# Scan products on 64-row tiles of the array with unpadded queries, and split ffn inputs moved in SBUF

## The chip, the cores and the metric

One core of a Trainium2 chip runs the whole program in one launch. The metric is device time in microseconds (us) of one execution: the median of the timed runs. A profiled execution gives the trace: a start and a duration for each instruction on TensorE (PE for matmuls, PEld for weight loads), VectorE (DVE), ScalarE (ACT), GpSimd (POOL) and SyncE (SP, which issues the DMAs).

## The reference

A two-layer backbone over 1024 latent tokens and 256 context tokens, width 1024, all in fp32. Layer 0 mixes tokens by attention and a convolution, layer 1 by a bidirectional RWKV-7 scan with 16 heads of 64; each layer ends in a SwiGLU channel mixer of hidden width 2816. What matters here is the scan and the mixer:

```python
def swiglu(h, w1, w3, w2):
    return (jax.nn.silu(h @ w1) * (h @ w3)) @ w2

def step(S, inp):                       # one token; per head a 64 x 64 state S
    w_t, k_t, v_t, kk_t, b_t = inp[:5]
    sa = jnp.einsum('bhvk,bhk->bhv', S, kk_t)
    S = S * w_t[:, :, None, :] - sa[..., None] * b_t[:, :, None, :] + v_t[..., None] * k_t[:, :, None, :]
    y = jnp.einsum('bhvk,bhk->bhv', S, inp[5]) if emit else None
    return S, y

for d in range(2):                      # forward and backward
    s_ctx, yc = wkv_scan(s0, dec_c, k_c, fc['vh'], fc['kk'], b_c, fc['r'], rev)
    _, yl = wkv_scan(s_ctx, dec_l, k_l, fl['vh'], fl['kk'], b_l, fl['r'], rev)
out_lat = rwkv_readout(y_lat[0] + y_lat[1], fl, p)   # group norm, bonus, gate, projection
```

## The kernel before, in words

**Order.** The program is written in a tile framework that allots buffers, inserts the waits, and orders the instructions of each engine from the order of the code together with its own model of their durations. The phases follow one another: the mixer of layer 0, its output projection (`mix_out`), `ffn(0)`, the projections of layer 1, `layer1_scan`, `mix_out(1)`, `ffn(1)`, `store`.

**Split products.** Large products are made in three passes: `split` makes a high part (ACT) and the remainder (DVE) of an operand, and `mm3` issues high x high, high x low and low x high (lines 59, 60 and 61). So `pf<-xh,whi` in a view is the first pass of an ffn product.

**ffn.** `ffn(l, ...)` runs over groups of two hidden blocks of 128. For each block and each token tile (`TT`: the context's 256 tokens, then two tiles of 512 latent tokens) the inputs `xh`, `xl` are multiplied with two 128-column blocks of w1 and w3 (tile `pf`); silu and product give `sl`, which is split into `gh`, `gl`; these are multiplied with w2 (also called `pf` in the views) and added to the residual `hT`. `operands(l, sizes)` allots `xh` and `xl` in a pool X0 or X1, opened before the weights' pools. In this allocation the rows of X0 and X1 begin 192 bytes past those of the weights, both taken mod 512 bytes; `gh` and `gl` lie in the weights' own pool, at distance 0. The `xh`, `xl` of 512 tokens are read in `mix_out` as well (tile `pw`).

**Scan.** The 16 heads are taken in 4 quarters Q of two head pairs (`pr`), each pair two heads (`h`) of 64. Per quarter there are five windows of 256 tokens (`g` = 0 is the context, without output; 1 to 4 the latent tokens), per window four chunks of 64 tokens (`m`), and both directions `d` run in turn. `HR[0]` and `HR[1]` are partitions 0 to 63 and 64 to 127: for most operands partitions hold the two heads of a pair, feature by feature.

- `prep_in` loads the window's operands by DMA and makes, on ACT, DVE and POOL, the scaled keys `kb` and the queries `qa` (for the correction inside a chunk) and `qz` (for the output). `qa` and `qz` are padded: for each chunk there are two blocks of 64 columns, one for each head, and the block of head h is zero on the partitions of the other. The zeros are written once (the memsets of line 1051); each window writes the two halves by one POOL op each (`pmul`, line 1056). `abp` is the 64x64 product of keys and queries that is inverted.
- `prep_mat` makes `kps`: keys by queries, 128 partitions contracted, with the zeros keeping the heads apart; then `l` on DVE (mask), and transposes of the keys (`tps` to `bk`).
- `prep_inv` inverts the triangular blocks, on DVE for the most part (lines 1203 and 1204), to `xc`.
- `scan` is the recurrence. For each chunk and direction: `px` (from `l` and the values `sv`, then from `qa` and the state `sc`), copied by ACT into `xs` with two ops (line 1267) into a block-diagonal form; `pu` = xc times xs, copied by ACT into `sv`; `pss` = new state, scaled on DVE to `sc`; then `py`, the output, from `qz` and `sc` and from `l` and `sv`. In `px` and `py` the two 64-column tiles of the array take the two pairs, each matmul contracting over all 128 rows.
- `readout` normalizes, adds the bonus (`vy`) and gates the output of a window, and transposes it by TensorE (`yps`).

The loop at the end of `layer1_scan` sets `scan` of window n beside the inversion and `kps` of window n + 1 and the loads of window n + 2, and up to two readouts.

Of the kernel before, what the change touches and what calls it, by code (L numbers as in the profile page):

```python
# [9 lines left out]
F32 = mybir.dt.float32  # L10
F32R = mybir.dt.float32r
# [32 lines left out]
class Kern:  # L44
# [942 lines left out]
    def layer1_scan(self, R, prepared):  # L987
# [5 lines left out]
        with ExitStack() as st:  # L993
# [52 lines left out]
            qas = [[U.tile([P, 8, 2, 64], F32, name=f"qa{d}{i}") for i in range(3)] for d in range(2)]  # L1046
            qzs = [[U.tile([P, 8, 2, 64], F32, name=f"qz{d}{i}") for i in range(2)] for d in range(2)]
            svs = [[U.tile([P, 2, 2, 2, 64], F32, name=f"sv{d}{i}") for i in range(2)] for d in range(2)]
            xs = [U.tile([P, 2, P], F32, name=f"xs{d}") for d in range(2)]
            for t in (xcs[0], xcs[1], xs[0], xs[1], *qas[0], *qas[1], *qzs[0], *qzs[1]):  # L1050
                nc.vector.memset(t, 0.0)
# [9 lines left out]
            def start_quarter(Q):  # L1061
# [9 lines left out]
                for pr in range(2):  # L1071
                    f0 = Q * 256 + pr * 128
                    nc.sync.dma_start(q.lg[HR[pr]].rearrange("p h v -> p (h v)"), I["rw_ln_g"][0][f0:f0 + 128].partition_broadcast(64))
# [3 lines left out]
            def prep_in(Q, q, g, n):  # L1077
# [34 lines left out]
                for d, u in enumerate(units):  # L1112
# [11 lines left out]
                    u.qa, u.qz = qas[d][n % 3], qzs[d][n % 2]  # L1124
                    for h in range(2):
                        pmul(u.qa[HR[h], :, h], rv(pprev)[HR[h]], rv(kkwin)[HR[h]])
# [23 lines left out]
                if lat:  # L1150
                    for u in units:
                        rw = u.win[2]
                        for h in range(2):
                            pmul(u.qz[HR[h], :, h], u.pcur[HR[h]], rw[HR[h]])
                        u.cq = S.tile([P, 8, 64], F32, tag="cq", name="cq", bufs=3)
                        pmul(u.cq, u.t, rw)

            def prep_mat(Q, q, g, units):
# [6 lines left out]
                for i in range(2):  # L1165
                    for d, u in enumerate(units):
                        hw, kb = i ^ d, u.kb
                        l = u.l[hw] = U.tile([P, 2, 4, P], F32, tag=f"l{d}", name="l", bufs=3)
                        for e in range(2):
                            m = 2 * hw + e  # L1170
                            ps = pk.tile([P, 4, P], F32, tag="k", name="kps")
                            for pr in range(2):
                                for c, x in ((0, u.qa), (64, u.qz))[:w // 64]:
                                    nc.tensor.matmul(ps[:, 2 * pr:2 * pr + 2, c:c + 64], kb[:, 4 * pr + m].rearrange("p a s -> p (a s)"), x[:, 4 * pr + m], start=True, stop=True)
                            nc.vector.tensor_tensor(l[:, e, :, :w], ps[:, :, :w], msk[d][:, :, :w].to_broadcast([P, 4, w]), op=ALU.mult)
# [16 lines left out]
            def prep_inv(units, par):  # L1192
# [38 lines left out]
                for d in range(2):  # L1231
                    units[d].xc = xc[:, 8 * d:8 * d + 8].rearrange("p (m h) s -> p m h s", h=2)
# [17 lines left out]
            def scan(Q, q, g, units):  # L1250
                lat = g > 0
                for j in range(4):
                    for d in range(2):
# [5 lines left out]
                        l = u.l[m // 2][:, m % 2]  # L1259
# [309 lines left out]
```

## Time and profile before

| | us |
|---|---|
| median of 3 timed runs | 4185.2 (4184.05 to 4185.81) |
| profiled execution, its own time | 4188.13 |
| its span in the trace | 4186.4 |
| PE busy | 3832.1 (92% of the span) |
| PEld busy | 3132.3 (75%) |
| DVE busy | 2403.9 (57%) |
| ACT busy | 1741.1 (42%) |
| POOL busy | 1161.3 (28%) |
| mean granted TensorE clock | 0.943 |

The stages as the trace has them, roughly: ffn of layer 0 from 970 to 1900, projections of layer 1 to 2405, scan from 2410 to 3345, output projection of layer 1 to 3430, ffn of layer 1 to 4170, store. How to read a line of the views: `L59 PE MATMUL pf<-xh,whi 128*128 128x512 f32` is line 59 of the kernel, on PE, writing pf from xh and whi, on a tile of 128 rows by 128 columns of the array, with an operand of 128 partitions by 512 columns. An fp32 matmul in the scan appears as two records; in the split products each pass is one. The duration of a matmul in the trace is a modelled one and overlaps its neighbours; the interval between starts says what one costs.

### The profile page before, as it was taken

What the parts mean: (1) busy time and instruction counts of PE and PEld (TensorE: products, weight loads), DVE (VectorE), ACT (ScalarE), POOL (GpSimd) and SP (SyncE); (2) the same over time, 40 slices, a digit from 0 to 9 for tenths busy, and PEclk for the clock granted to TensorE, in tenths of its full rate; (3) what the DMA queues carried; (4) which work ended last, traced back from release to release, by engine and by line L of the source; (5) the groups of instructions that cost most, each with busy time, mean ns of one, the idle gap of its engine ahead of it and who ended that gap; (6) DMA issues with size and microseconds to landing.
All of it is one profiled execution on the core that took longest, in us unless ns stands there. A gap on an engine that the chain in (4) does not pass through costs nothing. (4 is left out here: it accounts for less than half of the span.)

```text
span 4186.4 us, 70705 instructions
## 1 busy us (share of the span) xinstructions
PE 3832.1 (92%) x28764; PEld 3132.3 (75%) x28764; DVE 2403.9 (57%) x4577; ACT 1741.1 (42%) x3590; POOL 1161.3 (28%) x978
## 2 busy tenths in 40 slices
PE   8888899899999999997998979787887799999999
PEld 5665667688888888886887957676776578888887
DVE  5698776555333433338678378878787654333433
ACT  4446566643111111116667357666666442111111
POOL 2869554510000000004223164645544020000000
PEclk9898999999999999998999979898988899999999
DMA  4322222331111111113223222222222231111111
GB/s 174 125 86 69 74 92 72 109 109 46 41 39 33 40 41 41 36 36 99 74 95 102 79 85 70 80 70 78 75 62 65 85 111 51 46 45 51 51 46 56
DMA packets 301669, 297.07 MB, mean 71 GB/s; under 512 B 19408, under 2 KB 267872, under 8 KB 301344
## 3 DMA queue, kind: packets, MB, share of 16 engines
q1 hardware_dynamic: 293488, 277.07, 21.4%
q10 hardware_dynamic: 7056, 14.75, 1.0%
q8 instruction: 227, 3.72, 0.4%
q0 software_dynamic: 800, 0.73, 0.1%
q14 instruction: 98, 0.80, 0.1%
HBM read 246.36 MB, written 46.14 MB: 70 GB/s over the span
## 5 line engine op out<-in xcount | busy, mean ns | idle before, releaser
L59 PE MATMUL pf<-xh,whi 128*128 128x512 f32 (+1 forms) x1760 | 654.2, 372 | 0.0
L61 PE MATMUL pf<-xh,wlo 128*128 128x512 f32 (+1 forms) x1760 | 654.1, 372 | 0.0
L60 PE MATMUL pf<-xl,whi 128*128 128x512 f32 (+1 forms) x1760 | 653.8, 372 | 0.0
L54 ACT ACTIVATE whi<-raw 128x1024 fp32r<-128x1024 f32 (+1 forms) x207 | 214.8, 1049 | 909.3 <-PE pf L60 788.5
L55 DVE TENSOR_TENSOR wlo<-raw,whi 128x1024 fp32r<-128x1024 f32 (+1 forms) x207 | 270.1, 1314 | 259.6 <-ACT whi L54 254.9
L762 DVE SCALAR_TENSOR_TENSOR hT<-pf,mod,hT 128x512 f32<-128x512 f32 (+1 forms) x440 | 306.3, 697 | 196.3 <-PE pf L61 194.3
L751 DVE TENSOR_TENSOR sl<-sl,pf 128x512 f32<-128x512 f32 (+1 forms) x110 | 69.8, 635 | 581.2 <-PE pf L61 581.2
L61 PEld LDWEIGHTS pf<-xh,wlo 128*128 128x128 f32 x1760 | 330.8, 188 | 64.7
L60 PEld LDWEIGHTS pf<-xl,whi 128*128 128x128 f32 x1760 | 330.8, 188 | 64.5
L59 PEld LDWEIGHTS pf<-xh,whi 128*128 128x128 f32 x1760 | 330.6, 188 | 64.6 <-ACT xh L221 0.3
L60 PE MATMUL pf<-gl,whi 128*128 128x512 f32 (+1 forms) x880 | 324.1, 368 | 0.0
L61 PE MATMUL pf<-gh,wlo 128*128 128x512 f32 (+1 forms) x880 | 323.9, 368 | 0.0
L59 PE MATMUL pf<-gh,whi 128*128 128x512 f32 (+1 forms) x880 | 323.9, 368 | 0.0
L581 POOL TENSOR_TENSOR pl<-pe,pt 128x512 fp32r<-128x512 f32 (+1 forms) x176 | 226.4, 1297 | 190.8 <-PE po L60 103.0
L791 POOL MEMSET apad<- 128x8 f32 x4 | 0.2, 122 | 884.6 <-PE pf L61 884.6
L367 POOL TENSOR_TENSOR co<-co,cpr 128x655 f32<-128x655 f32 x90 | 193.8, 2154 | 46.6 <-ACT cpr L366 36.9
L54 ACT ACTIVATE gh<-sl 128x512 fp32r<-128x512 f32 (+1 forms) x110 | 64.9, 590 | 307.8 <-DVE sl L751 307.8
L59 PEld LDWEIGHTS pf<-gh,whi 128*128 128x128 f32 x880 | 165.9, 189 | 27.9
L60 PEld LDWEIGHTS pf<-gl,whi 128*128 128x128 f32 x880 | 165.9, 189 | 27.7
L61 PEld LDWEIGHTS pf<-gh,wlo 128*128 128x128 f32 x880 | 165.9, 189 | 27.6
L1203 DVE TENSOR_TENSOR tmp<-A,X 128x126 f32<-128x126 f32 (+22 forms) x620 | 154.0, 248 | 52.3 <-ACT X L1197 38.6
L354 DVE SCALAR_TENSOR_TENSOR co<-yp,parC,co 128x1310 f32<-128x1310 f32 (+1 forms) x90 | 177.0, 1967 | 1.5
(407 smaller groups left out, 9634.8 us busy)
## 6 DMA issues: line engine op xcount, KB each, us to landing
raw<-in_ffn_w_dram SPq DMA_DIRECT2D x132, 512.0 KB, 3.9
araw<-in_ada_w_dram SPq DMA_DIRECT2D x96, 512.0 KB, 4.5
low<-lod SPq DMA_DIRECT2D x40, 256.0 KB, 2.8
kw<-kd SPq DMA_DIRECT2D x40, 256.0 KB, 3.0
kkw<-kkd SPq DMA_DIRECT2D x40, 256.0 KB, 2.8
sv<-vd SPq DMA_DIRECT2D x80, 128.0 KB, 3.1
raw<-in_even_w_out_dram SPq DMA_DIRECT2D x16, 512.0 KB, 3.6
rw<-rd SPq DMA_DIRECT2D x32, 256.0 KB, 3.1
```

The costliest lines, as they stand in the source:

```text
L54: self.nc.scalar.activation(hi, src, AF.Copy)
L55: return self.nc.vector.tensor_tensor(lo, src, f32(hi), op=ALU.subtract)
L59: mm(ps, wh, xh, start=start, stop=False)
L60: mm(ps, wh, xl, start=False, stop=False)
L61: mm(ps, wl, xh, start=False, stop=stop)
L354: nc.vector.scalar_tensor_tensor(co, yp[:, w + c:w + c + n], cw(j, w), co, op0=ALU.mult, op1=ALU.add)
L367: nc.gpsimd.tensor_tensor(co, co, pr, op=ALU.add)
L581: nc.gpsimd.tensor_tensor(pl, pe, f32(pt), op=ALU.subtract)
L751: nc.vector.tensor_tensor(sl[:, :n], sl[:, :n], pp[1][:, :n], op=ALU.mult)
L762: nc.vector.scalar_tensor_tensor(hT[ti][:, mb], ps[:, :n], g[:, mb], hT[ti][:, mb], op0=ALU.mult, op1=ALU.add)
L791: nc.gpsimd.memset(ap[:, :, c:c + 1], 0.0)
L1203: nc.vector.tensor_tensor(tmp, A[:, k + 1:32, k:k + 1].to_broadcast([P, n, wd]), X[:, k:k + 1, 0:wd].to_broadcast([P, n, wd]), op=ALU.mult)
```

## The change

Scan:

- `qa`, `qz` and their zeros are replaced by one tile `q` per window and direction (three buffers): per chunk 64 columns of `qa` and 64 of `qz`, no padding. Each is written by one POOL op on 128 partitions in place of two on 64.
- A head's products contract over its own 64 rows: `kps` of the two heads goes to two PSUM banks through two 64x128 tiles, `abp` uses 64x32 tiles, the `q` products in `px` and `py` 64x64 tiles, `pu` 64x64 tiles. The products with `l` contract over 128 rows as before.
- Output partitions of `px`, `pu`, `py` and of the readout now stand for the head, not for the pair. So `xs` is one ACT op on 128 partitions, `yps` is made by 16 matmuls of 64x64 with a part of the identity in place of four transposes, and the loads of `vy` and of the norm's gain `lg` are four DMAs each in place of two.

ffn: `operands` puts a pad of 80 fp32 columns (modulo 128) ahead of the tiles of 512 tokens, so that their rows come to distance 0 from the weights mod 512 bytes; the tile of 256 tokens stays at 192.

The diff, cut:

```diff
-            qas = [[U.tile([P, 8, 2, 64], F32, name=f"qa{d}{i}") for i in range(3)] for d in range(2)]
-            qzs = [[U.tile([P, 8, 2, 64], F32, name=f"qz{d}{i}") for i in range(2)] for d in range(2)]
-            xs = [U.tile([P, 2, P], F32, name=f"xs{d}") for d in range(2)]
-            for t in (xcs[0], xcs[1], xs[0], xs[1], *qas[0], *qas[1], *qzs[0], *qzs[1]):
+            for t in xcs:
                 nc.vector.memset(t, 0.0)
...
-                for pr in range(2):
-                    f0 = Q * 256 + pr * 128
-                    nc.sync.dma_start(q.lg[HR[pr]].rearrange("p h v -> p (h v)"), ...)
+                for h in range(2):
+                    for pr in range(2):
+                        nc.sync.dma_start(q.lg[HR[h], pr], lng[h, pr].partition_broadcast(64))
...
-                    for h in range(2):
-                        pmul(u.qa[HR[h], :, h], rv(pprev)[HR[h]], rv(kkwin)[HR[h]])
+                    u.q = U.tile([P, 8, 2, 64], F32, tag=f"q{d}", name="q", bufs=3)
+                    pmul(u.q[:, :, 0], rv(pprev), rv(kkwin))
...
-                    for m in range(4):
-                        for b in range(4):
-                            i, c0 = 4 * (b // 2) + m, 32 * (b % 2)
-                            nc.tensor.matmul(ps[32 * b:32 * b + 32, 2 * m:2 * m + 2, 0:64 - c0], u.kb[:, i, 0, c0:c0 + 32], u.qa[:, i, :, c0:64], start=True, stop=True)
+                    for i in range(8):
+                        for b in (0, 2, 1, 3):
+                            r, c0, j = HR[b // 2], 32 * (b % 2), 2 * (i % 4) + i // 4
+                            nc.tensor.matmul(ps[32 * b:32 * b + 32, j, 0:64 - c0], u.kb[r, i, 0, c0:c0 + 32], u.q[r, i, 0, c0:64], start=True, stop=True)
...
-                        for h in range(2):
-                            pmul(u.qz[HR[h], :, h], u.pcur[HR[h]], rw[HR[h]])
+                        pmul(u.q[:, :, 1], u.pcur, rw)
...
-                        for e in range(2):
-                            m = 2 * hw + e
-                            ps = pk.tile([P, 4, P], F32, tag="k", name="kps")
-                            for pr in range(2):
-                                for c, x in ((0, u.qa), (64, u.qz))[:w // 64]:
-                                    nc.tensor.matmul(ps[:, 2 * pr:2 * pr + 2, c:c + 64], kb[:, 4 * pr + m]..., x[:, 4 * pr + m], start=True, stop=True)
-                            nc.vector.tensor_tensor(l[:, e, :, :w], ps[:, :, :w], msk[d]..., op=ALU.mult)
+                        pss = [pk.tile([P, 4, P], F32, tag="k", name="kps") for _ in range(2)]
+                        for j in range(4):
+                            c = 4 * (j % 2) + 2 * hw + j // 2
+                            for h in range(2):
+                                nc.tensor.matmul(pss[h][:, j, :w], kb[HR[h], c]..., u.q[HR[h], c]...[:, :w], start=True, stop=True)
+                        for h in range(2):
+                            nc.vector.tensor_tensor(l[:, h, :, :w], pss[h][:, :, :w], msk[d]..., op=ALU.mult)
...
-                        for h in range(2):
-                            for pr in range(2):
-                                nc.tensor.matmul(px[HR[pr], h], l[:, 2 * pr + h, 0:64], sv[:, pr, h], start=True, stop=False)
-                            for pr in range(2):
-                                nc.tensor.matmul(px[HR[pr], h], u.qa[:, 4 * pr + m, h], sc[:, pr], start=False, stop=True)
-                        for pr in range(2):
-                            nc.scalar.activation(xs[d][HR[pr], :, 64 * pr:64 * pr + 64], px[HR[pr]], AF.Copy)
-                            (pu: two matmuls of 128 columns)
+                        for pr in range(2):
+                            for h in range(2):
+                                nc.tensor.matmul(px[HR[h], pr], l[:, h, pr, 0:64], sv[:, pr, h], start=True, stop=False)
+                            for h in range(2):
+                                nc.tensor.matmul(px[HR[h], pr], u.q[HR[h], 4 * pr + m, 0], sc[HR[h], pr], start=False, stop=True)
+                        xs = U.tile([P, 2, 64], F32, tag=f"xs{d}", name="xs", bufs=2)
+                        nc.scalar.activation(xs, px, AF.Copy)
+                        for pr in range(2):
+                            for h in range(2):
+                                nc.tensor.matmul(pu[HR[h], pr], u.xc[HR[h], m, pr], xs[HR[h], pr], start=True, stop=True)
...
+                            for pr in range(2):
+                                for h in range(2):
+                                    nc.tensor.matmul(py[HR[h], pr], u.q[HR[h], 4 * pr + m, 1], sc[HR[h], pr], start=True, stop=False)
+                                for h in range(2):
+                                    nc.tensor.matmul(py[HR[h], pr], l[:, h, pr, 64:128], sv[:, pr, h], start=False, stop=True)
...
-                    nc.tensor.transpose(ps[:, m]..., yt[:, m]..., self.ident)
+                    for pr in range(2):
+                        for h in range(2):
+                            nc.tensor.matmul(ps[HR[h], m, pr], yt[HR[h], m, pr], self.ident[HR[h], HR[h]], start=True, stop=True)
...
-                xs_ = {i: [X.tile([P, KB, sizes[i]], F32R, name=f"x{k}{i}") for k in "hl"] for i in order}
+                xs_, at = {}, 0
+                for i in order:
+                    pad = ((80 if sizes[i] == 512 else 0) - at) % 128
+                    if pad:
+                        X.tile([P, pad], F32, name=f"pad{i}")
+                        at += pad
+                    xs_[i] = [X.tile([P, KB, sizes[i]], F32R, name=f"x{k}{i}") for k in "hl"]
```

More of the change, by code (lines that the diff above doesn't have):

```diff
@@ L1070, in start_quarter @@
                 q.lg = R.tile([P, 2, 64], F32, tag="lg", name="lg", bufs=2)
[L1071 to L1073 removed]
+                lng = I["rw_ln_g"][0][Q * 256:Q * 256 + 256].rearrange("(q h v) -> h q v", q=2, h=2)
+                for h in range(2):
+                    for pr in range(2):
+                        nc.sync.dma_start(q.lg[HR[h], pr], lng[h, pr].partition_broadcast(64))
                 q.y = {}
@@ L1231, in prep_inv @@
                 for d in range(2):
-                    units[d].xc = xc[:, 8 * d:8 * d + 8].rearrange("p (m h) s -> p m h s", h=2)
+                    units[d].xc = xc[:, 8 * d:8 * d + 8].rearrange("p (m q) s -> p m q s", q=2)
             cur = [None, None]
@@ L1258, in scan @@
                         sv = svt[:, m % 2]
[L1259 removed]
+                        l = u.l[m // 2][:, :, 2 * (m % 2):2 * (m % 2) + 2]
                         px = pc.tile([P, 2, 64], F32, tag=f"c{d}", name="px")
[L1261 to L1272 removed]
+                        for pr in range(2):
[5 more added lines that the diff above has]
+                        nc.scalar.activation(xs, px, AF.Copy)
+                        pu = pc.tile([P, 2, 64], F32, tag=f"c{d}", name="pu")
+                        for pr in range(2):
+                            for h in range(2):
+                                nc.tensor.matmul(pu[HR[h], pr], u.xc[HR[h], m, pr], xs[HR[h], pr], start=True, stop=True)
+                        for h in range(2):
+                            nc.scalar.activation(sv[0:64, :, h], pu[HR[h]], AF.Copy, scale=-1.0)
                         if not (g == 4 and j == 3):
@@ L1288, in scan @@
                             py = pc.tile([P, 2, 64], F32, tag="y", name="py")
-                            for h in range(2):
-                                for pr in range(2):
-                                    nc.tensor.matmul(py[HR[pr], h], u.qz[:, 4 * pr + m, h], sc[:, pr], start=True, stop=False)
-                                for pr in range(2):
-                                    nc.tensor.matmul(py[HR[pr], h], l[:, 2 * pr + h, 64:128], sv[:, pr, h], start=False, stop=True)
+                            for pr in range(2):
[3 more added lines that the diff above has]
+                                    nc.tensor.matmul(py[HR[h], pr], l[:, h, pr, 64:128], sv[:, pr, h], start=False, stop=True)
                             win = (tok - NCTX) // 256
@@ L1305, in readout @@
                 vy = R.tile([P, 4, 2, 64], F32, tag="vy", name="vy", bufs=1)
-                for pr in range(2):
-                    f0 = Q * 256 + pr * 128
-                    nc.sync.dma_start(vy[HR[pr]].rearrange("p m h v -> p m (h v)"), self.vd[NCTX + win * 256:NCTX + (win + 1) * 256, f0:f0 + 128].rearrange("(m t) f -> t m f", t=64))
+                vin = self.vd[NCTX + win * 256:NCTX + (win + 1) * 256, Q * 256:Q * 256 + 256].rearrange("(m t) (q h v) -> h q t m v", t=64, q=2, h=2)
+                for h in range(2):
+                    for pr in range(2):
+                        nc.sync.dma_start(vy[HR[h], :, pr], vin[h, pr])
                 gt = R.tile([P, 2, 256], F32, tag="gt", name="gt", bufs=1)
@@ L1326, in readout @@
                 for m in range(4):
-                    for pr in range(2):
-                        nc.tensor.matmul(ps[HR[pr], 2 * m:2 * m + 2], q.cr[win][:, 64 * m:64 * m + 64], selh[:, pr], start=True, stop=True)
+                    for h in range(2):
+                        nc.tensor.matmul(ps[HR[h], 2 * m:2 * m + 2], q.cr[win][:, 64 * m:64 * m + 64], selh[:, :, h], start=True, stop=True)
                 cf = R.tile([P, 8], F32, tag="cfs", name="cfs", bufs=2)
@@ L1336, in readout @@
                 for m in range(4):
-                    nc.tensor.transpose(ps[:, m].rearrange("p a t -> p (a t)"), yt[:, m].rearrange("p h v -> p (h v)"), self.ident)
+                    for pr in range(2):
+                        for h in range(2):
+                            nc.tensor.matmul(ps[HR[h], m, pr], yt[HR[h], m, pr], self.ident[HR[h], HR[h]], start=True, stop=True)
                 for pr in range(2):
```

9 lines of the change are left out of this document (2 added, 7 removed).

## The prediction, made before the change was timed

> **What bounds the kernel now.** I read the page from the top: the busy shares, the granted clock by slice, and the chain that ended last.
>
> ```profile
> span 4186.4 us, 70705 instructions
> ...
> PE 3832.1 (92%) x28764; PEld 3132.3 (75%) x28764; DVE 2403.9 (57%) x4577; ACT 1741.1 (42%) x3590; POOL 1161.3 (28%) x978
> ...
> PEclk9898999999999999998999979898988899999999
> ...
> PE pf L59 6%; PE pf L61 6%; PE pf L60 6%; DMA out_dram<-o 0%; PE t L1429 0%; PE cps L186 0%; ACT o L1431 0%; PE cpb L193 0%; DVE hT L762 0%; ACTq L1431 0%
> ```
>
> TensorE is busy 92% of the span, and the end is a chain of nothing but pf matmuls, the ffn of layer 1. That share is an average over stages, so I took busy time by stage: ffn of layer 0, the scan, ffn of layer 1. Columns: length, then PE, PEld, DVE, ACT, POOL busy, granted TensorE clock, DMA share, GB/s.
>
> ```profile
> 1000.00:1800.00 800.00, 800.00 (x4157) 679.95 (x4156) 290.50 (x409) 120.83 (x174) 0.00 (x0) 1.00 0.13 39
> 2410.00:3345.00 935.00, 758.57 (x12576) 626.09 (x12576) 727.78 (x2085) 589.93 (x1530) 443.49 (x401) 0.87 0.25 73
> 3500.00:4160.00 660.00, 660.00 (x2856) 534.44 (x2855) 237.85 (x294) 106.78 (x138) 0.00 (x0) 1.00 0.15 45
> ```
>
> In both ffn stages PE is never idle and the clock is whole: there the time is the sum of matmul intervals, and what an interval loses the kernel loses. The scan is otherwise: PE is idle for 935 - 759 = 176 us, DVE is busy 728, the clock is 0.87. It is a chain that hops between engines, and PE time there counts in part. The two halves of the change fall into these two kinds of stage.
>
> **The ffn operands, term by term.** Matmuls in order of start, each start and its modelled duration; the start-to-start interval is the price.
>
> ```profile
> 3691.49 0.39 PE L61 MATMUL pf<-gh,wlo 128*128 128x512 f32 x1
> ...
> 3703.05 0.39 PE L61 MATMUL pf<-gh,wlo 128*128 128x512 f32 x1
> 3703.27 0.39 PE L59 MATMUL pf<-xh,whi 128*128 128x512 f32 x1
> ...
> 3714.47 0.39 PE L59 MATMUL pf<-xh,whi 128*128 128x512 f32 x1
> ```
>
> From gh (the second product; gh lies in the weights' pool, its rows at distance 0 from them mod 512 bytes) 51 intervals take 11.56 us: 226.7 ns. From xh (rows 192 bytes past the weights) 48 take 11.20 us: 233.3 ns. Same shape, line and clock; the operand's place is what differs. The padding moves the 512-wide xh and xl to distance 0, so I price them like gh: 233.3 - 226.7 is 6.6 ns less, of which I take 6.4, as the starts are read to 10 ns. The number moved:
>
> ```profile
> L59 PE MATMUL pf<-xh,whi 128*128 128x512 f32 x1408 | 556.9, 396 | 0.0
> L59 PE MATMUL pw<-xh,whi 128*128 128x512 f32 x224 | 90.5, 404 | 3.5 <-ACT whi L54 3.5
> ```
>
> Three products each (lines 59, 60, 61): 3 x 1408 = 4224 in the ffns, 3 x 224 = 672 in the output projections, 4896 x 6.4 ns = 31 us. PE has no idle time there to swallow it: **-31 us** in full. Bounds: 0 if distance isn't the cause, -32 at 6.6 ns. The 256-wide context tile is left at 192, and there the order is the reverse: from gh 47 intervals take 5.63 us, 119.8 ns.
>
> ```profile
> 1040.07 0.28 PE L59 MATMUL pf<-gh,whi 128*128 128x256 f32 x1
> ...
> 1045.70 0.28 PE L61 MATMUL pf<-gh,wlo 128*128 128x256 f32 x1
> ...
> 1012.53 0.28 PE L59 MATMUL pf<-xh,whi 128*128 128x256 f32 x1
> ...
> 1017.64 0.28 PE L59 MATMUL pf<-xh,whi 128*128 128x256 f32 x1
> ```
>
> From xh 45 take 5.11 us, 113.6. So the distance isn't simply good or bad, and leaving this tile where it is costs nothing.
>
> **The scan.** Its groups: records, busy us, mean ns, idle time before and its releaser (an fp32 matmul shows as two records).
>
> ```profile
> L1174 PE MATMUL kps<-qa,kb 128*128 128x128 f32 x640 | 147.4, 325 | 22.3 <-DVE l L1175 15.4 <-ACT cr L1190 4.4 <-ACT bk L1181 2.0
> L1174 PE MATMUL kps<-qz,kb 128*128 128x128 f32 x512 | 110.8, 302 | 2.7 <-POOL qz L1056 2.7
> L1267 ACT ACTIVATE xs<-px 64x128 f32<-64x128 f32 x320 | 86.9, 272 | 87.2 <-PE px L1265 81.8 <-ACT xs L1267 0.4
> L1056 POOL TENSOR_TENSOR qa<-pp,kkw 64x512 f32<-64x512 f32 x79 | 95.0, 1202 | 24.6 <-ACT pp L1118 20.8 <-DMA sv<-vd 0.7
> L1056 POOL TENSOR_TENSOR qz<-pp,rw 64x512 f32<-64x512 f32 x64 | 84.4, 1320 | 84.3 <-PE py L1291 82.1
> L1056 POOL TENSOR_TENSOR kp<-kkw,pi 128x512 f32<-128x512 f32 x39 | 51.2, 1313 | 3.8 <-DVE gneps L1025 1.1
> ```
>
> And the stretch that prices a record and a change of tile:
>
> ```profile
> 2603.79 0.39 PE L1174 MATMUL kps<-qz,kb 128*128 128x128 f32 x2
> 2604.01 0.39 PE L1174 MATMUL kps<-qa,kb 128*128 128x128 f32 x2
> 2604.33 0.34 PE L1291 MATMUL py<-sc,qz 128*64 128x64 f32 x4
> 2604.49 0.29 PE L1293 MATMUL py<-sv,l 128*64 128x64 f32 x4
> 2604.61 0.29 PE L1291 MATMUL py<-sc,qz 128*64 128x64 f32 x4
> ```
>
> *kps, gain.* Two records take 0.22 us, so 640 + 512 = 1152 take 127 us. Afterwards the padding's zero half is gone: two matmuls on 64-row tiles, in two PSUM banks, do in one pass what took two. If the tiles run side by side, half goes: **-63 us of PE time**; if not, 0.
>
> *Change of tile, cost.* The two kps records begun at 2604.01 would be done at 2604.23; py, on 128x64 tiles, starts at 2604.33, and its first four records take 0.16 where the next four take 0.12. That is 0.10 + 0.04, about 0.145 us, for one change of tile shape. The nearest row for a change of row tile:
>
> ```profile
> 1986.35 0.28 PE L61 MATMUL p3m<-mh,wlo 128*128 128x256 f32 x1
> 1986.56 0.38 PE L915 MATMUL p3b<-rh,hexp 16*128 16x256 f32 x1
> 1986.78 0.28 PE L916 MATMUL p3b<-rl,hexp 16*128 16x256 f32 x1
> 1986.99 0.39 PE L59 MATMUL p3m<-mh,whi 128*128 128x256 f32 x1
> 1987.21 0.28 PE L60 MATMUL p3m<-ml,whi 128*128 128x256 f32 x1
> 1987.33 0.28 PE L61 MATMUL p3m<-mh,wlo 128*128 128x256 f32 x1
> ```
>
> Five intervals take 0.98 where five of the usual 0.118 would be 0.59: 0.39 more for two changes, 0.19 each. Afterwards l keeps 128x64 tiles while the q product takes 64x64, in turn: px goes l, q, l, q (3 changes within), py goes q, l, q, l (3). There are 4 quarters x 5 windows x 4 chunks x 2 directions = 160 px and 128 py, so 3 x 288 = 864 changes where none were: x 0.145 = **+125 us of PE time**. I take 0.145, from tiles of the same width; bounds 0 (no row shows 128x64 against 64x64) and 0.19, +164. Beside that pu becomes 64x64 and pss stays 128x64: at most one more change in each of 160 steps, +23, kept for the upper end.
>
> The Trainium skill, page "TensorEngine Tiling (Array Packing)", section "Key Properties", says that changing the tiling mode, not just the tile, drains the TensorE, which speaks against this change; the trace agrees by the 0.145 and 0.19 above. By that rule all 864 are paid, which is rival C's 4252 if none of it is hidden; by the lower bound none is, which is rival B's 4145.
>
> *Smaller PE terms.* yps: 4 transposes become 16 matmuls of two records.
>
> ```profile
> L1337 PE MATMUL yps<-ident,yw 128*128 128x128 f32 x64 | 10.9, 296 | 2.2 <-DVE yw L1333 2.1
> ...
> 2662.61 0.69 PE L1228 MATMUL gp<-xc,gz 32*32 32x32 f32 x32
> ```
>
> Four transposes at 0.11 are 0.44 us; 32 records, four in 0.117 as in py, are 0.93: +0.5 x 16 = +8. abp has twice the matmuls of half the length: the same columns. If issue bounded it, 1280 more records at the 0.69 / 32 = 0.0216 us of the smallest tiles are +28; I take 0, since the column stream sets the interval elsewhere. pu doubles its matmuls and halves their columns: 0.
>
> *Sum on PE:* -63 + 125 + 8 = +70 at full clock, /0.87 = +80. *What reaches the end:* at least nothing (176 us of PE idle could take it), at most all. px sits on the recurrence (ACT's xs waits 81.8 us on it), yet work of the other direction fills much of a wait; I take half: **+40**.
>
> *ACT.* xs becomes one op of 128 partitions: 320 x 0.272 to 160 x 0.272, -43 us of ACT. The pair's second op lies on the recurrence, and half of its pairs overlap other waits; 80 serial steps x 0.272 = 22 bounds it; the PE changes are late next, and with the other direction running beside it I take a quarter: **-6**.
>
> *DVE and POOL.*
>
> ```profile
> L1051 DVE MEMSET qa<- 128x1024 f32 x6 | 5.5, 912 | 5.9 <-PE p3m L61 5.2 <-issue 0.7
> ...
> 2404.91 0.87 SPq L1091 DMA_DIRECT2D rw<-rd  x2
> ```
>
> Ten memsets of 0.912 us go, ahead of the scan on DVE; they run while the first chunk is loaded and projected: **-3**, bounds 0 and -9. POOL: a half op takes as long as a whole one (1.2 to 1.3 us, kp 1.31), so 80 + 64 ops become 40 + 32, about -90 us. Nothing but 2.7 us of kps waits on qz, so this is hidden: 0. The 82.1 us that qz waits for py goes too, with three buffers for both halves; kb's wait for its own buffer is late next on POOL, and nobody waits for POOL there.
>
> *DMA issues.* vy 32 to 64, lg 8 to 16, half as large, on SP: 40 more at 0.87 / 2 = 0.44 us, 18 us of SP over 935, ahead of the sv and window loads in the queue. These are issued a chunk or more ahead: 0, at worst some us.
>
> **Sum.** -31 + 40 - 6 - 3 = 0 against the profiled execution's own 4188.1 us (span 4186.4 and 1.7 around it). The median of the timed runs is 4185.2, 3 us lower; so **4185 us**.
>
> **Rivals.** (B) *The changes of tile are hidden.* PE idles 176 us in the scan, and the drain may overlap the wait that follows anyway; or 128x64 to 64x64 doesn't drain. Then PE's terms give nothing or a gain: -31 - 9 = -40, 4145; with half the kps share also reaching the end (-63 / 0.87 / 2 = -36), 4109. For it: the idle time, and DVE's 728 us as the other bound. Against: the 0.10 that py waited in the middle of ready work. (C) *The changes are paid in full*, since each px is on the recurrence of its direction and both directions make them: (70 + 23) / 0.87 = 107, less 9, less 31: +67, 4252. It decides against the change once more than (31 + 9) / 107 = 37% of the added PE time reaches the end. For it: xs's wait on px. (D) *The two row tiles of kps don't run side by side*, so that half isn't saved: PE +133 / 0.87 / 2 = +76 instead of +40, 4221. No row here shows two 64-row tiles at once; 32x32 tiles do run so (32 records in 0.69 us). (E) *Distance isn't the cause* of the 6.4 ns: 31 lost, 4216. Against: the two intervals stand side by side in one stage at one clock, with the same shape.
>
> The Trainium skill, page "TensorE: Matmul & The Clock Gate", Part 3, has four row tiles of K=32 run concurrently at 3.07 times the speed of one after the other; no run here shows it. By it D falls.
>
> **How the numbers follow.** A (half reaches the end) 0.46, 4185, its own range 4155 to 4215 (from a tenth to nine tenths of the 80 us); B 0.28; C 0.16; D 0.05; E 0.05. 0.2%, 8.4 us, is about what timing can tell from no change. Of A a third falls below 4176.8, a third above 4193.6. Faster: 0.15 + 0.27 = 0.42. Slower: 0.16 + 0.15 + 0.08 = 0.39. Same: the rest, 0.19. The range leaves out a tenth at each end: within B up to the values with some kps gain, 4120, and C's 4250.
>
> **What would show it.** The xh interval of the ffns at 227 ns, both ffn stages 31 us shorter together; anything near 233 means E. In the scan: kps records half in number at 0.11 us per pair of tiles (else D); intervals of 0.2 us and more at each l-q alternation in px and py (else B); PE busy near 759 + 80; the scan some 31 us longer, 67 for C, unchanged or shorter for B; xs 160 ops. The prediction is wrong most likely in the half that I chose: the order of the instructions is made anew for the changed program, and it may set the two directions' products side by side so that alternations vanish, or spread them and add some.

## The result and the profile after

The changed kernel takes 4582.9 us (median of 4 runs, 4560.2 to 4591.2) against 4184.6 of the kernel before on the same chip: 1.094 times as long, 95% interval 1.090 to 1.098. The forecast was 4185, and the range ended at 4250.

The page of the changed kernel: span, busy time, the busy share of PE by slice, and the granted TensorE clock by slice.

```profile
span 4576.7 us, 75276 instructions
...
PE 4343.4 (95%) x31260; PEld 3539.1 (77%) x31260; DVE 2410.3 (53%) x4565; ACT 1698.0 (37%) x3428; POOL 1071.8 (23%) x906
...
PE   8888998899999999799898999999999989999999
...
PEclk9888998999999999899995557555557679999999
```

Read the two slice rows together. From slice 22 to 33, the scan, PE is busy nearly all the time, and the clock is near half: 5 for most, where the scan of the kernel before had 7 to 9. The stages (columns as before: length, PE, PEld, DVE, ACT, POOL busy, clock, DMA share, GB/s):

```profile
2410.00:3745.00 1335.00, 1291.46 (x14970) 1020.78 (x14962) 737.32 (x2068) 547.14 (x1366) 342.95 (x325) 0.58 0.17 49
1000.00:1800.00 800.00, 800.00 (x4194) 690.70 (x4193) 293.48 (x415) 120.86 (x175) 0.00 (x0) 1.00 0.13 39
3850.00:4500.00 650.00, 650.00 (x2870) 538.27 (x2870) 254.35 (x329) 116.86 (x157) 0.00 (x0) 1.00 0.16 49
```

From its first abp to its last py the scan grew from 924 to 1336 us, +412; all the rest shrank from 3262 to 3240 (the spans of the two traces, 4186.4 and 4576.7, less their scans). PE's idle time in the scan went from 176 us to 44, yet it had fewer clock pulses: 935 us at 0.87 are 813 us of full clock, 1335 at 0.58 are 774. The array got no more cycles than before and needed 400 us more to get them. DVE's work hardly changed (737 us, 728 before); ACT's and POOL's fell by 43 and 101, about as forecast.

The ffn, two stretches of matmuls, each in order of start:

```profile
4103.13 0.39 PE L59 MATMUL pf<-xh,whi 128*128 128x512 f32 x1
...
4111.97 0.39 PE L59 MATMUL pf<-xh,whi 128*128 128x512 f32 x1
...
1015.61 0.28 PE L59 MATMUL pf<-xh,whi 128*128 128x256 f32 x1
...
1019.85 0.28 PE L59 MATMUL pf<-xh,whi 128*128 128x256 f32 x1
```

With 512 columns thirteen rounds of three passes take 8.84 us: 226.7 ns an interval, where xh had 233.3. With 256 columns twelve rounds take 4.24 us: 117.8 ns, where xh had 113.6. This tile's distance from the weights mod 512 bytes was left at 192, and it lost 4.2 ns all the same; 3 x 352 such matmuls in the ffns cost 4.4 us.

The scan at full clock (one of its short spells), and at half clock (start, duration, operation, records):

```profile
3522.80 1.16 PE L1171 MATMUL kps<-q,kb 64*128 64x128 f32 x8
...
3523.89 0.27 PE L1290 MATMUL py<-sc,q 64*64 64x64 f32 x2
...
3528.02 0.34 PE L1261 MATMUL px<-sv,l 128*64 128x64 f32 x4
3528.28 0.33 PE L1263 MATMUL px<-sc,q 64*64 64x64 f32 x4
3528.55 0.34 PE L1261 MATMUL px<-sv,l 128*64 128x64 f32 x4
...
3258.86 2.07 PE L1171 MATMUL kps<-q,kb 64*128 64x128 f32 x8
3260.86 0.48 PE L1261 MATMUL px<-sv,l 128*64 128x64 f32 x4
3261.27 0.48 PE L1263 MATMUL px<-sc,q 64*64 64x64 f32 x4
3261.68 0.48 PE L1261 MATMUL px<-sv,l 128*64 128x64 f32 x4
```

At full clock px takes 0.26 or 0.27 us for four records, where it took 0.117: about 0.145 for a change of tile, the price forecast. At half clock it takes 0.41, of which some 0.21 is stream. Eight kps records take 1.09 us with a change at the end, some 0.12 a record without it; run 1 below gives 0.112 for one row tile alone and 0.056 for two side by side. The group of kps has 1280 records, more than the 1152 of before: 1024 of 128 columns, shown here, and 256 of 64 columns, busy 53.2 us. Together that is 294 us, where the two groups of before had 258. The second line is the copy of px to xs, one op in place of two:

```profile
L1171 PE MATMUL kps<-q,kb 64*128 64x128 f32 x1024 | 241.1, 416 | 2.9 <-ACT bk L1179 2.1 <-DVE l L1173 0.8
...
L1265 ACT ACTIVATE xs<-px 128x128 f32<-128x128 f32 x160 | 44.1, 277 | 131.5 <-PE px L1263 130.1
```

The order of PE's instructions explains it: of the 640 kps matmuls, most stand as four of head 0 and later four of head 1 (a matmul of the one head follows one of the other directly only 114 times). The pool has two PSUM banks for kps and tps. The reading is that the second head's bank was not yet free when the first head's four were ready, so that these were set ahead by themselves; run 6, which allots both banks at once, bears it out. Rows of one half then work alone.

### The profile page after: what moved, and what is told of

The parts are those of the page before. It is cut to its first block, busy times and chain, and to the rows that moved or that the text cites. A ratio compares the mean times of both kernels' runs of the same rounds, so it can differ in the third digit from the quotient of the medians.

```text
span 4576.7 us, 75276 instructions
## 1 busy us (share of the span) xinstructions
PE 4343.4 (95%) x31260; PEld 3539.1 (77%) x31260; DVE 2410.3 (53%) x4565; ACT 1698.0 (37%) x3428; POOL 1071.8 (23%) x906
## 5 line engine op out<-in xcount | busy, mean ns | idle before, releaser
L1171 PE MATMUL kps<-q,kb 64*128 64x128 f32 (+1 forms) x1280 | 294.3, 417 | 2.9 <-ACT bk L1179 2.1
L1171 PEld LDWEIGHTS kps<-q,kb 64*128 64x128 f32 x1280 | 236.3, 295 | 30.9 <-issue 8.3
L1173 DVE TENSOR_TENSOR l<-kps,msk 128x512 f32<-128x512 f32 (+1 forms) x160 | 100.2, 633 | 171.0 <-PE kps L1171 170.2
```

The lines of the kernel that those rows point to most:

```text
L1171: nc.tensor.matmul(pss[h][:, j, :w], kb[HR[h], c].rearrange("p a s -> p (a s)"), u.q[HR[h], c].rearrange("p a s -> p (a s)")[:, :w], start ...
L1173: nc.vector.tensor_tensor(l[:, h, :, :w], pss[h][:, :, :w], msk[d][:, :, :w].to_broadcast([P, 4, w]), op=ALU.mult)
```

## The experiments

Theory R: the clock is granted by the rows at work, so 64-row tiles lower it. Theory S: the changes of tile lower it, since each empties the array. Each `scan` figure below is from the first abp to the last py of the profiled execution. The changes of tile are counted in the same stretch, in the order of the starts in the trace: 642 in the kernel before, 1963 in the changed one.

**1. Stretches of one kind, begun at full clock.** A kernel with nothing but matmuls; the heart of three of its stretches:

```python
for i in range(160):   # kps now, heads in turn
    mm(ps[i % 2][:, c(i // 2)], w[HR[i % 2], c(i // 2)], x[HR[i % 2], c(i // 2)], start=True, stop=True)
for i in range(600):   # 64x64 on the diagonal
    mm(ps[0][HR[i % 2], f(i // 2)], w[HR[i % 2], f(i // 2)], x[HR[i % 2], f(i // 2)], start=True, stop=True)
for i in range(400):   # px now: two on 128x64, two on 64x64
    r = slice(0, 128) if i // 2 % 2 == 0 else HR[i % 2]
    mm(ps[0][HR[i % 2], f(i // 2)], w[r, f(i // 2)], x[r, f(i // 2)], start=True, stop=True)
```

> This kernel does nothing of the reference: it runs ten stretches of fp32 matmuls, each after about 20 us of full-array ones, and writes a placeholder. Stretches in order: 128x128 tiles; kps's new form (two 64x128 tiles in turn, two banks); one 64x128 tile alone; px's old form (two 128x64 tiles); two 64x64 tiles on the diagonal, no change of tile; px's new form (two matmuls on 128x64, two on 64x64, in turn); the same in groups of four; all four 64x64 tiles; two 64x128 tiles with 512-column one-pass operands. Theory R (the clock is granted by how much of the array is at work, so that a 64-row tile counts half): the granted clock is 1.0 in the 128-row stretches and falls to 0.5 in every stretch made of 64-row tiles, above all in the pure diagonal one. Theory S (the clock falls because each change of tile empties the array): 1.0 in all pure stretches, 0.5 only in the two that alternate, 128x64 with 64x64. Kps's new form: if the two tiles run side by side, 0.055 us a record; if not, 0.11.

The first eight of these stretches, in the order named (columns as before):

```profile
47.60:80.60 33.00, 33.00 (x297) 32.96 (x297) 0.00 (x0) 0.00 (x0) 0.00 (x0) 1.00 0.01 1
98.90:116.80 17.90, 17.90 (x319) 17.86 (x320) 0.00 (x0) 0.00 (x0) 0.00 (x0) 1.00 0.01 3
135.30:171.10 35.80, 35.80 (x321) 35.73 (x320) 0.00 (x0) 0.00 (x0) 0.00 (x0) 1.00 0.01 1
189.60:224.70 35.10, 35.10 (x1201) 35.04 (x1200) 0.00 (x0) 0.00 (x0) 0.00 (x0) 1.00 0.02 4
243.10:278.20 35.10, 35.10 (x1201) 35.04 (x1200) 0.00 (x0) 0.00 (x0) 0.00 (x0) 1.00 0.02 4
296.60:349.20 52.60, 52.60 (x801) 39.14 (x800) 0.00 (x0) 0.00 (x0) 0.00 (x0) 1.00 0.01 2
367.70:405.60 37.90, 37.90 (x801) 31.15 (x800) 0.00 (x0) 0.00 (x0) 0.00 (x0) 1.00 0.01 3
424.10:446.60 22.50, 14.84 (x800) 14.10 (x800) 0.00 (x0) 0.00 (x0) 0.00 (x0) 0.88 0.02 4
```

Neither theory held: the clock stayed at 1.0 in the first seven, the alternating ones too. Only the eighth, all four 64x64 tiles, fell to half clock after 17 us; PE is shown busy for 14.84 of its 22.5 us. The lengths are good prices, though. Heads in turn, 320 kps records take 17.9 us, 0.056 each; one tile alone 35.8, 0.112. Pairs on 128x64 and pairs on 64x64 cost the same, 0.0292 a record; the two in alternation 0.0657. So four records on average cost 0.146 more for a change.

**2. The padding alone.** The kernel before with the last part of the diff only.

> Only the padding of the ffn operands; the scan is as before. The distance theory: xh and xl intervals of the ffns go from 233 to 227 ns, -31 us, 4153 to 4156. Rival (distance is not the cause): intervals stay at 233, 4184.

4157.1 against 4184.3: ratio 0.993 (0.991 to 0.995); the scan is as it was, 923 us at clock 0.88, and the rest 28 us shorter; the interval of xh at 512 columns is 227 ns here too. So the place of the operands is the cause, and it is worth what was forecast, within the interval; the 27 us are the forecast 31 less the 4.4 that the tile of 256 columns lost. Whether the distance from the weights decides, or the operand's own place, no run separates.

**3. kps on 64-row tiles alone.** In the kernel before:

```diff
-  nc.tensor.matmul(ps[:, 2 * pr:2 * pr + 2, c:c + 64], kb[:, 4 * pr + m]..., x[:, 4 * pr + m], ...)
+  for h in range(2):
+      nc.tensor.matmul(pss[h][:, 2 * e + pr, c:c + 64], kb[HR[h], k]..., x[HR[h], k, h], ...)
```

> The kernel before, with kps alone on two 64x128 tiles (from the unpadded blocks of the padded queries); px, py and everything else as before, so no changes of tile within px and py. Theory R: kps, a sixth of the scan's PE time, counts half; the scan's clock falls from 0.87 to some 0.75 to 0.8 and the scan grows by 30 to 90 us. Theory S: no more changes of tile than before; clock 0.85 to 0.9, time within 15 us of 4184.

4331.7: ratio 1.035 (1.033 to 1.038), worse than theory R asked, with no change of tile inside px and py.

```profile
2410.00:3486.00 1076.00, 995.06 (x13712) 841.86 (x13712) 736.92 (x2071) 586.31 (x1524) 435.65 (x394) 0.78 0.21 61
```

In this form kps has 64 columns per matmul and 1152 matmuls, each with its own weight load, where the changed kernel has 640; here too most stand one head at a time. Within the full-clock spells such a record of 64 columns takes 0.112 us, as one of 128 columns did before, and there are twice as many: so the run isn't a test of the rows alone. Its 64 columns stream on half of the rows for about half of that time. The changes of tile rise from 642 to 1017, as kps no longer shares its shape with the transposes and projections around it, so S is not excluded.

**4. px and py on 64-row tiles alone.** The changed layout, with kps and abp on 128 rows from padded queries.

> The changed scan's layout with kps and abp on 128 rows from padded queries as before, and only the q products of px and py (and pu) on 64x64 tiles, alternating with l on 128x64; no padding of the ffn operands. Theory S: the 864 changes of tile are all there, so the clock falls to 0.55 to 0.6 as in the changed kernel and the scan takes 1270 us or more: 4520 or more. Theory R: kps counts in full again, so the clock recovers in part, to 0.65 to 0.8, and the scan takes 1050 to 1200 us: 4300 to 4450.

The kernel that ran did have the padding of the ffn operands, other than the expectation says, so its measure is the 4157 of run 2. 4307.3, +150; ratio to the kernel before 1.029 (1.027 to 1.031).

```profile
2401.00:3472.00 1071.00, 977.62 (x14866) 791.90 (x14868) 720.80 (x2071) 542.10 (x1366) 431.30 (x394) 0.80 0.21 62
```

Theory S, which gave it the whole loss, falls; R's numbers held. Each half costs some 150 us by itself, run 3's with its extra loads, and both together 426: more than the sum.

**5. The same stretches, begun at half clock.** As run 1, with some 12 us of an idle array ahead of each.

> Does nothing of the reference: nine stretches of fp32 matmuls, each begun after some 15 us in which the array idles (VectorE copies), so at half clock. In order: 128x128 tiles; kps in pairs of 64x128 tiles; one 64x128 tile alone; 64x128 tiles in turn by fours (the order that the changed kernel got); 128x64 pairs (px before); 64x64 pairs on the diagonal; 128x64 and 64x64 in turn by two (px now); by four; all four 64x64 tiles. Theory R (a low clock rises only when the work of a window fills enough of the array, and 64-row tiles that run alone or in one pair count half): the clock rises to 1.0 within some us in the first, second, fifth and last stretch, and stays at 0.5 for the whole of the others, the pure diagonal one and the single tile among them. Theory S (emptying at a change of tile keeps it low): it rises in all but the seventh and eighth. A third possibility, that any unbroken stretch raises it: 1.0 in all.

Its stages in the order named (columns: length, PE, PEld, DVE, POOL busy, clock, DMA share, GB/s):

```profile
18.20:88.00 69.80, 69.78 (x600) 69.78 (x600) 0.00 (x0) 0.00 (x0) 1.00 0.00 1
99.90:147.50 47.60, 47.55 (x800) 47.55 (x800) 0.00 (x0) 0.00 (x0) 0.94 0.01 2
159.40:244.80 85.40, 85.35 (x400) 85.35 (x400) 0.00 (x0) 0.00 (x0) 0.50 0.00 1
256.80:287.70 30.90, 30.84 (x400) 30.84 (x400) 0.00 (x1) 0.00 (x0) 0.90 0.01 2
299.60:348.30 48.70, 48.63 (x1600) 48.63 (x1600) 0.02 (x1) 0.00 (x0) 0.96 0.02 4
360.10:409.70 49.60, 49.45 (x1600) 49.27 (x1600) 0.04 (x1) 0.00 (x0) 0.95 0.01 4
421.50:503.40 81.90, 81.85 (x800) 58.53 (x800) 0.00 (x0) 0.00 (x0) 0.50 0.01 1
515.30:577.50 62.20, 62.16 (x800) 50.55 (x800) 0.00 (x0) 0.00 (x0) 0.50 0.01 2
589.40:633.40 44.00, 29.39 (x1600) 27.83 (x1600) 0.00 (x0) 0.00 (x0) 0.91 0.02 4
```

This is the reading on which the rest stands. Three stretches never left half clock, though PE is shown busy without a gap for 62 to 85 us: one 64x128 tile alone, and 128x64 in turn with 64x64, by two and by four. Theory R missed twice: pairs of 64x64 on the diagonal rise (all 128 rows are at work), and kps by fours rises too. S missed the single tile, which changes nothing.

What divides them is for what share of the time all rows stream. The single tile gives the price of a record at half clock: 85.35 us for 400 records of 128 columns, 0.213 each; one of 64 columns takes half, and two such run side by side, 0.053 each. By two, a record took 81.9 / 800 = 0.102, so the array is filled for 0.52 of the time; by four 62.2 / 800 = 0.078, 0.69; the single tile has half the rows, 0.5. These three stay low. Kps by fours took 0.137 a record in the last 3.4 us before the clock rose, as neighbouring fours overlap in part: 0.213 / 2 / 0.137 = 0.78. That one rises. So at half clock the array must be filled for more than some 0.7 to 0.78 of a clock window (3.41 us, the unit of which all spells in the clock records are multiples). **Theory U**: kps one head at a time (0.5) and px and py in alternation (0.52) both stay below, whatever their order, so a scan that has dropped to half clock stays there; at full clock the same instructions hold the clock (run 1), since a window then holds twice the work.

The kept traces show where the clock falls, too. As an estimate, each matmul record is given its streaming time at full clock (half of the 0.213 us above for 128 columns) times its share of the rows, divided by the number of column tiles that share these rows; the sum in a clock window, as a share of the window, is its row work. In the 3748 whole windows of the scans of before, after and runs 2 to 4 and 6 to 12, the next window is at full clock in all 1545 cases with more than 0.42 of row work, and in 30 of the 1387 with less than 0.32. One level for both directions, 0.36, is right for 95% of the windows; the best level for PE's busy share is wrong for 37% of them. A half-clock window can hold 0.5 at most, so 0.36 there is the array filled for 0.72 of the time. The stretches of runs 1 and 5 fit. The single tile makes 0.48 at full clock and 0.25 at half, the alternation by two 0.41 and 0.26, that by four 0.56 and 0.34, and kps by fours 0.39 in its last window at half. So kps one head at a time and px and py in alternation hold full clock as long as PE seldom waits, and once a wait has dropped them they can't rise by themselves. The eighth stretch of run 1 fell after a window with 0.35.

**6. kps in pairs.** In the changed kernel:

```diff
-  pss = [pk.tile([P, 4, P], F32, tag="k", name="kps") for _ in range(2)]
+  k2 = pk.tile([P, 2, 4, P], F32, tag="kk", name="kps")
+  pss = [k2[:, h] for h in range(2)]
```

The pools of zps and abp, and of kps and tps, then have one buffer of each kind in place of two.

> The changed kernel with kps of both heads in one buffer of two PSUM banks, so that the order of the instructions sets the two row tiles side by side (one bank less for zps and abp, one for tps). Theory R: kps takes 0.056 us a record again and fills the array; scan clock up from 0.57 to 0.65 to 0.85, time 4250 to 4450. Theory S: only the 63 us of kps at full clock are gained, 110 at half; about as many changes of tile as before it; clock stays below 0.62: 4450 to 4520.

4424.3 (ratio to before 1.057, 1.054 to 1.061), 159 less than the changed kernel, within R's range and past S's.

```profile
2398.00:3586.00 1188.00, 1104.41 (x15000) 866.92 (x14991) 718.05 (x2068) 537.80 (x1362) 337.00 (x325) 0.66 0.20 56
```

```profile
L1172 PE MATMUL kps<-q,kb 64*128 64x128 f32 x1024 | 142.6, 380 | 24.5 <-DVE l L1174 17.1 <-DVE tmp L1202 4.2 <-DVE X L1203 3.1
```

The group takes 142.6 us where it took 241.1. The changes of tile are nearly as many as before (1921 against 1963), and a kps matmul of one head now follows one of the other 461 times.

**7. One change within px and py in place of three.** In the changed kernel: both pairs' products with l first, then both with q (py the other way round).

> The changed kernel with px and py issuing both pairs' l products and then both pairs' q products (py the other way round), so one change of tile within each in place of three; nothing else differs. Theory S: with a quarter fewer changes (in the order of the instructions 1370 against 1840) the clock recovers in part, 0.65 to 0.8: 4250 to 4450. Theory R: the rows in use are the same, and only the time of the changes is saved, 480 x 0.145 = 70 us at full clock, up to 130 at half: 4450 to 4520, clock below 0.65.

4348.2 (1.039, 1.036 to 1.043), 235 less; S's range, and more than the time of the changes saved. Counted as above the changes are 1418 against 1963 (the expectation has another count).

```profile
2397.00:3522.00 1125.00, 1045.07 (x15000) 859.10 (x14990) 725.96 (x2068) 543.44 (x1368) 337.11 (x325) 0.71 0.20 59
```

So R alone falls too; both mechanisms lower the same filled share.

**8. Padding, and kps alone in pairs, px and py on 128 rows.**

> The kernel before with the padding, and kps alone on two 64x128 tiles held in one buffer of two banks, px and py on 128 rows. If what hurt in kps alone (+147 us) was that the two tiles ran one after the other: the kps time halves, -63 us of PE at full clock, the clock is back at 0.85 or more, time 4110 to 4160. If 64-row tiles hurt as such: still 100 us and more above the padding alone (4157), 4260 or more.

4293.2 (1.027, 1.025 to 1.029): +136 on the padding alone, near the +147 of run 3. The expected gain failed, and "one after the other" is not what hurt here.

```profile
2399.00:3458.00 1059.00, 903.45 (x13712) 739.85 (x13712) 723.79 (x2071) 584.45 (x1524) 427.13 (x394) 0.77 0.21 62
```

The padded source allows 64 columns per matmul only, so kps has 2304 records, each matmul with its own load of 128 weight columns; in its full-clock spells a record in pairs takes 0.056 us, as long as one of 128 columns in run 1, and nothing is saved. At half clock it takes 0.107 us where two such run side by side at 0.053 in run 5, so the array is filled for half of the time, as with one head alone. There are 1069 changes of tile against 642. How much of the 136 us is that, how much those, and how much the narrower set of banks (one for zps and abp in place of two), stays open.

**9. What is left of the change when all q products use 128 rows.**

> The changed kernel's layout, with kps, abp and the q products of px and py all on 128 rows from padded queries as before; what is left of the change is the padding of the ffn operands, pu on 64x64 tiles, one copy of 128 partitions for xs, yps in 16 parts and the split DMAs. Theory U (the stretches with half the rows in use and the changes of tile together keep the array's filled share too low at half clock): kps and px/py are the cause, so the clock is 0.80 to 0.87 and the time 4150 to 4220, against 4157 of the padding alone. Rival: pu's tiles, the copies or the DMAs cost much by themselves, 4250 or more.

4171.6 (0.998, 0.997 to 0.999), some 15 to 20 more than the padding alone; the scan's clock is 0.90, a little above U's range.

```profile
2399.00:3334.00 935.00, 781.40 (x14864) 664.21 (x14854) 717.36 (x2068) 537.36 (x1368) 436.18 (x394) 0.90 0.24 70
```

The new layout with its single copy, pu on 64x64, yps in 16 parts and the split DMAs costs that little, though ACT is relieved of 50: no gain, no great loss. The memsets of the padded queries stay in this run. From here to the changed kernel lie 411 us: the 64-row tiles of kps, abp, px and py, with their unpadded queries.

**10. The changed kernel with more work.** After every second step, eight 128x128 matmuls into a bank that nobody reads:

```diff
+  for i in range(8 if d == 0 and Q * 5 + g < 19 else 0):
+      nc.tensor.matmul(dum[:, 0:P], self.ident, dmy, start=True, stop=True)
```

> The changed kernel with added work: after every second step of the scan eight 128x128 matmuls that write a bank nobody reads, 152 / 2 x 8 x 0.22 = 134 us of TensorE at full clock, twice that at half (and one bank less for zps and abp). Theory U: the added full-row work lifts the share of filled time in its windows, the clock rises more often, 0.65 to 0.8 in the scan, and the kernel with more work is faster than the changed one: 4400 to 4520. Rival (the clock follows the length of waits, or the scan's order, and not the work): the added work costs its time, 4650 to 4850, clock 0.57 or less.

4418.5 (1.057, 1.054 to 1.059): 608 matmuls more, and 164 us less than the changed kernel.

```profile
2403.00:3584.00 1181.00, 1160.13 (x16174) 947.28 (x16174) 712.80 (x2069) 539.80 (x1362) 343.38 (x325) 0.83 0.19 56
```

The time at half clock in the scan fell from 1128 us to 410, and its clock of 0.83 is above U's 0.65 to 0.8. The order of the other work became no better: 2033 changes of tile against 1963, and the heads of kps follow each other directly 130 times against 114. Useless full-row work made the kernel faster; nothing else that the trace shows can pay for it. This is the run that shows the clock to be the cause, not a companion.

**11. Both repairs, pairs and grouping.**

> Both repairs in the changed kernel: kps in pairs of row tiles, and one change of tile within px and py in place of three. Alone they gave 4424 and 4348 against 4583. Theory U: the two add up or more, since each lifts the same share of filled time: scan clock 0.78 or more, 4190 to 4270. If they only repaired the same windows: 4320 to 4350.

4336.8 (1.037, 1.034 to 1.040), 11 below the grouping alone: theory U's sum was wrong, and the time is the rival's, that they repair the same windows. The scan's clock is not higher, either:

```profile
2397.00:3499.00 1102.00, 971.12 (x14998) 786.00 (x15000) 717.32 (x2068) 535.61 (x1362) 337.80 (x325) 0.70 0.20 60
```

PE is idle for 131 us now where it was for 80 in run 7. Another reading is that with one buffer for kps, one for tps and one for zps and abp the engines wait more for each other, and idle time lowers the filled share as well. No run separates the two.

**12. Filler on the padding alone**, to see whether the scan's remaining 222 us at half clock can be bought back.

> The padding alone (4157 us, scan clock 0.88, 222 us of the scan at half clock) with three added 128x128 matmuls after each step of the scan that write a bank nobody reads: 152 x 3 x 0.22 = 100 us of TensorE at full clock, into a stage where it idles some 170 us; one bank less for zps and abp. Theory U: fewer windows fall to half clock; if the added work fits in the idle time, half of the 222 us at half clock goes, worth up to 50 us: 4110 to 4150. Rival: the clock rises but the added matmuls stand ahead of the next step's px in the queue, and the bank that is missing costs too: 4160 to 4230.

4193.2 (1.002, 1.001 to 1.003), 36 more than the padding alone, though the clock rose:

```profile
2400.00:3345.00 945.00, 818.32 (x13384) 695.53 (x13383) 715.62 (x2062) 592.20 (x1523) 447.13 (x397) 0.92 0.24 69
```

This line ends before the last py, at 3360: the whole scan takes 956 us at 0.92, with 150 us at half clock, where the padding alone took 923 with 222. The rival held: the higher clock didn't pay for 100 us of matmuls ahead of px and for the missing bank; which of the two costs more stays open. The best version found is the padding alone, 4157 us.

A form with l on 64x64 tiles as well, which would remove the changes within px and py without padding, was not tried.

## Why the prediction was wrong, point by point

- **The ffn, -31 us: right for the tiles of 512 columns.** They take 226.7 ns in the trace. That leaving the tile of 256 columns at 192 costs nothing was wrong: it went from 113.6 to 117.8 ns, 4.4 us in the ffns, and the padding alone gave -27 (run 2). Its distance mod 512 bytes didn't change, so this distance alone doesn't set the interval there; what does stays open.
- **A change of tile, 0.145 us: right in price**, at full clock; 0.146 in run 1, and some 0.2 at half clock. 128x64 against 64x64, which no row of before showed, costs the same as the pairs that it did show. The number was too low: 642 changes became 1963, so 1321 more, where 864 were counted and 160 for pu kept for the upper end. Between run 9 with 855 and run 4 with 1696 lie the q tiles of px and py, 841, near the 864; the rest comes with pu and the new layout and with kps and abp. At 0.145 all 1321 are 192 us of PE, not 125.
- **kps, -63 us: not obtained.** Rival D's outcome, by another cause than it named: 64x128 tiles do run side by side (0.056 in run 1), but the order of the instructions kept the heads apart. The banks were what the step had to look at: kps now needs two of a pool of two that tps uses as well.
- **The sum on PE, "/0.87": the step that failed.** I carried the granted clock of the old scan over as a constant and asked only which share of the added PE time would reach the end. The clock is a result of what PE does. It went to 0.58, and at 0.58 a scan of 774 us of full-clock cycles takes 1335. The terms that were mis-sized don't explain it: with kps at 0 and the changes at 192 the sum is 200 us, 230 after the division, and even paid in full that falls short of the 412 us that the scan lost. Rival C, the changes paid in full, went in the right direction, with +67 for the whole kernel.
- **Half reaches the end; 176 us of idle as cover.** The idle time was no cover: at half clock PE needs it itself, and 44 us of it are left.
- **xs, POOL, memsets, DMAs.** 160 copies, 44 us in place of 87; POOL 101 us less; neither is felt. The layout without the memsets' removal is worth +15 to +20 (run 9), where -6 was forecast for xs and +8 of PE time for yps; the -3 for the memsets was not tested.

The row that could have warned was in the prediction: the scan's clock of 0.87, a mean of spells at 1.0 and at 0.5. By the count of windows behind run 5, a stage whose clock is between the two has windows on both sides of the level, and the question to ask of any change there is whether it fills the array more or less of the time.

The Trainium skill, page "TensorE: Matmul & The Clock Gate", Part 1, has the clock in two states, half and full, set by how busy the array was in a window of about 3.4 us. The traces agree: the spells in the clock records are all multiples of 3.41 us, at 0.5 or 1.0, and the row work of one window decides the next. By its rule, that about one busy window raises the clock, a scan with PE busy 97% would run at full clock if busy meant PE's busy share; the traces disagree with that meaning, with 85 us of gapless single-tile matmuls at 0.5. The Trainium skill, page "TensorEngine Tiling (Array Packing)", section "Key Properties", has a drain at a change of tiling mode; the runs agree in that a change costs 0.146 us (run 1).

## What to carry to other kernels

Before pricing PE work in a stage, read its granted clock, and where it is neither 1.0 nor 0.5 ask how the change moves the share of time in which all rows stream: tiles with half the rows, and alternating tile shapes, lower it even while PE looks busy. Two row tiles side by side save half only if the order of the instructions keeps them adjacent, and that hangs on both having a free PSUM bank at once. Moving operands by some hundred bytes was worth 27 us: look at the interval between starts of like matmuls with different operands, and read it again afterwards for every tile that moved.

## What the runs showed of the hardware that was not expected

- From half clock, an array shown busy without a gap stays at half clock for as long as it is filled for 0.69 of the time or less (62 to 85 us, run 5), and rises in one to two windows at 0.78 and above; begun at full clock, the same stretches hold it (run 1). In the scans one level serves both ways: the next window is at full clock above some 0.36 of a full-clock window's row work (an estimate, right for 95% of 3748 windows).
- Two 64x64 tiles on the diagonal count as a full array in this, one 64x128 tile does not.
- Useless full-row work shortened a kernel by 164 us (run 10).
- With a moving operand of 512 columns an interval is 226.7 ns at distance 0 from the weights mod 512 bytes and 233.3 at 192. With 256 columns it is 119.8 at distance 0 (gh), but 113.6 before and 117.8 after at the same distance of 192 (xh): there this distance doesn't settle it.
